# A hybrid RWKV-7 and short-convolution block on one NeuronCore: one pair's recurrence outputs on other array quadrants, weight casts with a higher scheduling priority, and mix splits spread over projection tiles

## The chip, the cores and the metric

The kernel runs on one core of one Trainium2 chip. The metric is the device time of one execution in microseconds (us). The core's engines are named as the profile names them: PE (TensorE, the matmul engine; its weight loads are listed as PEld), DVE (VectorE), ACT (ScalarE), POOL (GpSimd) and SP (SyncE, which here issues nearly all DMAs). A small q behind a name (SPq) means the engine's instruction queue.

## What is computed

The input is 512 tokens of width 2048, with 16 learned tokens put in front (528 rows). The layer normalises the rows, multiplies them by `w_in` (2048 x 8320), and feeds two head groups: 16 RWKV-7 heads of 64 channels, and a gated width-3 convolution over 1024 channels. Cut to what matters:

```python
hn = _rmsnorm(h_res, norm_in_g[l]);  P = hn @ w_in[l]
# RWKV-7 group: token shift, then r, k, v, g_r, decay and a from P
def step(S, inp):                       # per head, S is 64 x 64
    r_t, w_t, k_t, v_t, kk_t, b_t = inp
    sa = einsum('bhvk,bhk->bhv', S, kk_t)
    S = S * w_t[..., None, :] - sa[..., None] * b_t[..., None, :] + v_t[..., None] * k_t[..., None, :]
    return S, einsum('bhvk,bhk->bhv', S, r_t)
yn  = groupnorm_per_head(y) * lnx_g + lnx_b
y_a = (yn + bonus) * silu(g_r)
# convolution group
y_b = Bg * causal_conv3(Cg * hc, conv_w[l]) * silu(g_c)
h_res = h_res + concatenate([y_a, y_b]) @ w_out[l]
out = _rmsnorm(h_res, norm_f_g)[:, 16:]
```

All inputs and the output are float32.

## The kernel before, in words

**Precision.** Every large matmul operand is split into a high part (a cast to fp32r) and a low remainder, and each product is made of three matmuls: high x high, high weight x low input, low weight x high input.

**Weights.** `prefetch` (L130) walks through one list of half tiles, `stream`: the 65 column tiles of `w_in` in the order of `plan`, then `w_out`. For each it takes a raw buffer `wr` (three of them), issues one DMA of 512 KB on SP (L134), and calls `split_w` twice, once per quarter of 512 columns. `split_w` (L123) casts on ACT (`wh`, L126) and subtracts on DVE or POOL (`wl`, L127: POOL takes every second quarter). There are six buffers each for `wh` and `wl`, so a cast waits until PE has done with the quarter six places earlier, and a raw buffer is free again when both its remainders are made.

**Projection.** `mains` (L448) is a Python generator that issues the projection's matmuls (L314) one by one; a tile takes 96 (for k, r, v, g, C and h) or 48 (for B and gc) matmuls in four quarters. After each tile `use` (L376) puts the vector work behind it: scaling, token shift, gates, the convolution. The last tiles of the plan are C, h, B and gc for convolution groups 4 to 7.

**What sets the order.** PE's order is written out by hand: the program's order is PE's order. `fill(ns)` (L500) draws matmuls from the generator until their costed length reaches `ns`, so that other PE work (the preparation, the recurrence) is laid between stretches of projection; `until` (L510) draws until a named tile is done. The lengths are in the table `FW` (L42). `later(ns, fn)` (L481) holds a DMA back until that many costed ns of projection have been drawn, and puts it behind the last weight DMA on SP. On ACT, DVE, POOL and SP a scheduler chooses the order when the program is built: by a cost model of its own it takes, among the instructions that are ready, the one earliest in the program. A block under `tc.high_priority(offset=n)` counts as if it stood n instructions earlier. Once chosen, the order on each engine is fixed, and an engine waits at an instruction whose operands are late, with all behind it. `ahead()` (L532) is such a block with the offset `AHEAD` (600); it holds the few copies that PE needs soon (`pn`, `u`, `st`, and the low-rank tanh and the solve's copies).

**Preparation.** The 16 heads are eight pairs of two. `prepare(i)` (L568) makes a pair's operands: two low-rank products `tz` and `ta` (L514), then `tz + 1` on DVE (L580), a scan `cc` (L582), two exponentials, the products `te`, `bk` (L590, L601) and `ar` (L597, L606), squares and splits (`sq_h`, `rk_h`, L550). PE then makes the Gram matrices `g` (L624). A triangular 16 x 16 solve of 72 blocks runs on DVE (`prod`, `tt`, `y`, L717 to L732); `y` goes to DRAM by a DMA held back by `later` (L747) and comes back as `xT` and `xo` (L738, L739). `invert` (L770) finishes two pairs' inverses (`t`, L790, is its first PE step). The operands of every pair and chunk go to DRAM (`opd`).

**Recurrence.** `recur` (L873) runs over nine chunks (chunk 0 holds the 16 learned tokens); all matmuls in it are 64 x 64 and take one quadrant of the array. For each chunk: `rz` part 0/1 (L887) into two PSUM buffers `z[0]` and `z[1]` of a pool of two, a negated copy `pn` (L895), the solve's product into the second half of the same buffers (L904), its copy `u` (L907, L908), and then two lists of matmuls laid alternately: `here` (L932), the state update `zs`, whose rows and columns of the array are the same half (the diagonal quadrants), 16 items; and `there` (L936), the output `zy`, whose columns are the other half (the off-diagonal quadrants), 24 items, three for each pair. An item is two matmuls, one per head. Then DVE makes the new state (`st`, L942, L943), `norm` (L950) normalises the outputs (DVE L958, L959, L962, L967, ACT L961, POOL L963 and L101, transpose L968) and a `later` puts them into DRAM (`yd`, L972). `fill(p)`, `fill(u)` and `fill(s)` lay projection matmuls between the steps.

**Mix splits and output.** `split_mix(j)` (L996) makes the 16 operand tiles of the output projection. For j below 8 it loads `rb`, `gg` (three buffers each) and two halves of `mr` (four buffers) from `yd` by SP (L1003, L1004, L1007), does two DVE steps (L1010), a cast on ACT (L1015) and a remainder on DVE (L1016). For j from 8 it loads `mr` from `mixd` (L1014), which `use` wrote after the gc tile. Before, `recur` is followed by `fill(last)` of 14000 ns, the held DMAs, and then by a loop over j = 0 to 15: the first eight with no projection between them, the others each after the tile gc j - 8 is done. The output projection (L1054) follows, four column blocks, and the tail (L1141 on) has its order by hand.

Of the kernel before, what the change touches and what calls it, by code (L numbers as in the profile page):

```python
# [9 lines left out]
F32 = mybir.dt.float32  # L10
# [3 lines left out]
ALU = mybir.AluOpType  # L14
AX = mybir.AxisListType
# [3 lines left out]
P = 128  # L19
DM = 2048  # L20
KT = DM // P
# [3 lines left out]
CH = 64  # L25
NCH = SEQ // CH + 1
LP = NCH * CH
NPAIR = 8
# [13 lines left out]

FW = dict(
    evac=34, start=1062, lora=2200, gram=8000, gram_b=13500, gram2=4800, gram3=3500, misc=2000, v=2000, vt=1000, solve=22500, solve_first=26000,
    tr=3200, lev=3000, cp=4200, out=1500, begin=17000, p=2900, u=2900, s=5200, last=14000,
)


AHEAD = 600


def _constants():
# [24 lines left out]
def hymba_kernel(ctx: ExitStack, tc: tile.TileContext, xt, xtok, w_in, w_out, pv, lup, cst, msk, gf, out):  # L77
    nc = tc.nc
# [44 lines left out]
    def split_w(q, rq, eng):  # L123
        hi = wp.tile([P, 512], F32R, tag="hi", name=f"wh{q}", bufs=6)
        lo = wp.tile([P, 512], F32R, tag="lo", name=f"wl{q}", bufs=6)
        nc.scalar.copy(hi, rq)  # L126
        eng.tensor_tensor(out=lo, in0=rq, in1=hi.bitcast(F32), op=ALU.subtract)  # L127
        quarters[q] = (hi, lo)

    def prefetch(upto):  # L130
        while state["next"] < min(upto, len(stream)):
            j = state["next"]
            raw = wp.tile([P, 1024], F32, tag="raw", name=f"wr{j}", bufs=3)
            state["dma"] = nc.sync.dma_start(raw, stream[j]).ins  # L134
            for q in range(2):
                split_w(2 * j + q, raw[:, q * 512 : (q + 1) * 512], nc.gpsimd if q and j > 8 else nc.vector)
            state["next"] = j + 1

    keep = ctx.enter_context(tc.tile_pool(name="keep", bufs=1, side="right"))
# [37 lines left out]
    raw = {}  # L177
# [390 lines left out]
    def prepare(i):  # L568
# [8 lines left out]

        tz = low_rank(i, 0, up, hv[:, 0, i : i + 1], f"tz{i}", -1.0)
        ta = low_rank(i, 1, up, hv[:, 1, i : i + 1], f"ta{i}", 0.0)
        nc.vector.tensor_scalar(out=tz, in0=tz, scalar1=1.0, scalar2=None, op0=ALU.add)  # L580
        cc = tr(f"cc{i}")
        nc.vector.tensor_tensor_scan(cc, smask.rearrange("p c s -> p (c s)"), tz, 0.0, op0=ALU.mult, op1=ALU.add)  # L582
        nc.gpsimd.memset(e1[:, :, 0:1], 1.0)
# [289 lines left out]
    def recur(ch):  # L873
        ops = {}
        load_chunk(ch, 0, range(NPAIR), ops)
        load_chunk(ch, 1, range(NPAIR), ops)
        st = None
        for c in range(NCH):
            last = c == NCH - 1
            z = [pz.tile([P, 2, 4, CH], F32, tag="tz", name=f"rz{c}_{e}") for e in range(2)]  # L880
            for k in range(4):
                for part in range(0 if c else 1, 2):
                    for e in range(2):
                        t = ops[c, 2 * k + e]
                        o = O_KK if part else O_AR
                        for h, hs, ho in heads:
                            nc.tensor.matmul(  # L887
                                z[e][ho if e else hs, 0, k], t[hs, o : o + CH],
                                t[hs, O_V : O_V + CH] if part else st[hs, 4 * e + k],
                                start=(part == 0 or c == 0), stop=(part == 1),  # L890
                            )
            pn = ch.tile([P, 2, 4, CH], F32, tag="pn", name=f"pn{c}", bufs=2)
            with ahead():
                for e in range(2):
                    nc.scalar.activation(pn[:, e], z[e][:, 0], AF.Copy, scale=-1.0)  # L895
            if c and not last:
                load_chunk(ch, c + 1, range(0, 4), ops)
            fill(FW["p"])
            for k in range(4):
                for e in range(2):  # L900
                    t = ops[c, 2 * k + e]
                    for h, hs, ho in heads:
                        m = ho if e else hs
                        nc.tensor.matmul(z[e][hs, 1, k], t[m, O_X : O_X + CH], pn[m, e, k], start=True, stop=True)  # L904
            u = ch.tile([P, 2, 4, CH], F32, tag="u", name=f"u{c}", bufs=2)
            with ahead():
                nc.scalar.copy(u[:, 0], z[0][:, 1])  # L907
                nc.vector.tensor_copy(u[:, 1], z[1][:, 1])  # L908
            if c and not last:
                load_chunk(ch, c + 1, range(4, NPAIR), ops)  # L910
            fill(FW["u"])
            here, there = [], []
            if not last:
                zs = pi.tile([P, NPAIR, CH], F32, tag="misc", name=f"zs{c}")
            if c:
                zy = pi.tile([P, NPAIR, CH], F32, tag="ser", name=f"zy{c}")
            for k in range(4):
                for e in range(2):
                    t, j = ops[c, 2 * k + e], 4 * e + k
                    if not last:  # L920
                        here += [(zs, j, t, O_B, u[:, e, k], 0, 2), (zs, j, t, O_K, t[:, O_V : O_V + CH], 1, 2)]
                    if c:
                        there += [
                            (zy, j, st[:, j], O_AR + CH, t, 0, 3),
                            (zy, j, t[:, O_V : O_V + CH], O_KK + CH, t, 1, 3),
                            (zy, j, u[:, e, k], O_BR, t, 2, 3),
                        ]
            for n in range(max(len(here), len(there))):
                if n < len(here):
                    d, j, t, o, x, a, b = here[n]  # L930
                    for h, hs, ho in heads:
                        nc.tensor.matmul(d[hs, j], t[hs, o : o + CH], x[hs], start=(a == 0), stop=(a == b - 1))  # L932
                if n < len(there):
                    d, j, x, o, t, a, b = there[n]
                    for h, hs, ho in heads:
                        nc.tensor.matmul(d[ho, j], t[hs, o : o + CH], x[hs], start=(a == 0), stop=(a == b - 1))  # L936
            if not last:
                new = ch.tile([P, NPAIR, CH], F32, tag="st", name=f"st{c}", bufs=2)
                scale = dd[:, c].unsqueeze(2).to_broadcast([P, NPAIR, CH])
                with ahead():  # L940
                    if c:
                        nc.vector.tensor_tensor(out=new, in0=zs, in1=st, op=ALU.add)  # L942
                    nc.vector.tensor_tensor(out=new, in0=new if c else zs, in1=scale, op=ALU.mult)  # L943
                st = new
            if c:
                norm(ch, zy, c)
            fill(FW["s"])


    def norm(ch, zy, c):  # L950
        nv = ch.tile([P, 4, NPAIR], F32, tag="nv", name=f"nv{c}", bufs=2)
        yc = ch.tile([P, NPAIR, CH], F32, tag="yc", name=f"yc{c}", bufs=2)
        yt = ch.tile([P, NPAIR * CH], F32, tag="yt", name=f"yt{c}", bufs=2)

        def spread(j):
            return nv[:, j].unsqueeze(2).to_broadcast([P, NPAIR, CH])

        nc.vector.tensor_reduce(out=nv[:, 0], in_=zy, op=ALU.add, axis=AX.X)  # L958
        nc.vector.scalar_tensor_tensor(out=yc, in0=spread(0), scalar=-1.0 / CH, in1=zy, op0=ALU.mult, op1=ALU.add)  # L959
        yq = yt.rearrange("p (j s) -> p j s", s=CH)  # L960
        nc.scalar.activation(yq, yc, AF.Square)  # L961
        nc.vector.tensor_reduce(out=nv[:, 1], in_=yq, op=ALU.add, axis=AX.X)  # L962
        nc.gpsimd.tensor_scalar(  # L963
            out=nv[:, 2], in0=nv[:, 1], scalar1=1.0 / CH, scalar2=LNX_EPS, op0=ALU.mult, op1=ALU.add
        )
        rsqrt(nv[:, 3], nv[:, 2])
        nc.vector.tensor_tensor(out=yc, in0=yc, in1=spread(3), op=ALU.mult)  # L967
        nc.vector.transpose(yt, yc.rearrange("p j s -> p (j s)"))  # L968

        def put():  # L970
            for b in range(4):
                nc.sync.dma_start(  # L972
                    bass.AP(
                        tensor=yd.tensor,
                        offset=yd.offset + (b // 2) * NPAIR * CH * SEQ + (c - 1) * CH + 32 * (b % 2),
                        ap=[[SEQ, 32], [32 * SEQ, 2 * NPAIR], [1, 32]],
                    ),
                    yt[32 * b : 32 * b + 32].rearrange("p (t s) -> p t s", s=32),
                )

        later(10500, put)
# [4 lines left out]
    ph2.close()  # L986
    with tc.tile_pool(name="ch", bufs=1, side="right", reuse_waits="tile") as ch:
        recur(ch)
        fill(FW["last"])
        run_pending(float("inf"))  # L990

    pp = ctx.enter_context(tc.tile_pool(name="pp", bufs=1, side="right", reuse_waits="tile"))
    order = list(range(KT))
# [2 lines left out]
    def split_mix(j):  # L996
# [3 lines left out]
        if j < NPAIR:  # L1000
# [2 lines left out]
            nc.sync.dma_start(rb, rbd[j])  # L1003
            nc.sync.dma_start(gg, gated[j])  # L1004
            for h, hs, ho in heads:
                o = (h * NPAIR + place[j]) * CH
                nc.sync.dma_start(raw[hs], yd[o : o + CH])  # L1007

            for x, w, z, o in ((raw, 0, rb, ALU.mult), (raw, 1, gg, ALU.add)):
# [5 lines left out]
        nc.scalar.copy(mh, raw)  # L1015
        nc.vector.tensor_tensor(out=ml, in0=raw, in1=mh.bitcast(F32), op=ALU.subtract)  # L1016

    for j in order:
        if j >= NPAIR:
            while ("gc", j - NPAIR) not in ready:  # L1020
                step()
        split_mix(j)
    for _ in flow:
        pass
# [194 lines left out]
```

## Time and profile before

| | |
|---|---|
| median of 3 runs | 1066.87 us (1066.67 to 1069.53) |
| the profiled execution, its time | 1066.87 us |
| the profiled execution, its span (first to last instruction) | 1065.1 us |
| granted TensorE clock, mean | 0.994 |
| PE busy | 98% of the span |
| instructions | 23993 |
| DMA, bytes moved | 167.49 MB, mean 157 GB/s |

The profile comes from one execution. In its timelines a row gives start, length (us), engine, line, operation and tiles, the number of merged instructions, and in brackets how long the engine stood idle before it and who released it. In the list of waits a row gives the waiting engine, tile and line, what it waited for, and the total, the number and the longest. In the chain of waits a row is start, length and what the chain went through. In the windows a row is the stretch, its length, then busy time and instruction count of PE, PEld, DVE, ACT and POOL, the granted clock (1.00 is full), the DMA engines' busy share and GB/s. In the answer for one line or one tile a row gives the shortest, median and longest duration in ns, and the first and last start. One fp32 matmul leaves two rows' worth of records, so a 64 x 64 item of two matmuls counts as four. "issue" stands for time in which an engine waited for nothing that the profile shows.

### The profile page before, as it was taken

The page shows a single profiled execution, that of the slowest core. Times are in us where ns is not written, and L with a number is a line of the kernel's source. Part 1 is how long each engine was busy: PE and PEld are TensorE (multiplying, and loading weights), DVE is VectorE, ACT ScalarE, POOL GpSimd, SP SyncE. Part 2 cuts the span into 40 slices and gives each one's busy share as a digit, 9 for nine tenths or more (in the row PEclk, how much of TensorE's full clock was granted, in tenths as well). Part 3 has the DMA queues.
Part 4 walks back from the last instruction along what each step waited for, and adds up shares of the span by engine and source line. Part 5 has one row for each costly group of instructions (what it writes and reads, how often), then busy time and mean ns, then how long its engine had stood idle before and what let it go on. Part 6 is the DMA issues. An engine that isn't in the chain of part 4 may idle for free.

```text
span 1065.1 us, 23993 instructions
## 1 busy us (share of the span) xinstructions
PE 1040.0 (98%) x9973; PEld 950.0 (89%) x9973; DVE 557.2 (52%) x1064; ACT 367.7 (35%) x682; POOL 292.4 (27%) x307
## 2 busy tenths in 40 slices
PE   8999999999999999999999999999999899999996
PEld 6999998999998999989999989898898878888885
DVE  6784964758553767644676552355444842212132
ACT  6553422533233443233443232222222342323232
POOL 0121323223132222231222231323223142424232
PEclk9999999999999999999999999999999999999999
DMA  8455564455653366643457638676745958333314
GB/s 291 137 136 138 142 169 133 128 132 144 172 152 113 107 169 145 147 141 112 124 127 173 176 108 312 215 243 188 224 104 147 244 184 315 82 96 99 99 60 158
DMA packets 182894, 167.49 MB, mean 157 GB/s; under 512 B 120961, under 2 KB 143233, under 8 KB 182401
## 3 DMA queue, kind: packets, MB, share of 16 engines
q1 hardware_dynamic: 182208, 164.90, 54.7%
q8 instruction: 78, 1.28, 0.5%
q10 hardware_dynamic: 576, 1.07, 0.3%
q14 instruction: 32, 0.25, 0.1%
HBM read 129.05 MB, written 36.88 MB: 156 GB/s over the span
## 4 chain that ended last, share of the span: by engine, by line
PE 91%; DVE 3%; DMA 2%; issue 1%; ACT 1%; SPq 0%; POOL 0%; DVEq 0%; ACTq 0%; POOLq 0%
PE o L1054 17%; PE ps_g L314 9%; PE ps_k L314 9%; PE ps_B L314 8%; PE ps_r L314 8%; PE ps_v L314 8%; PE ps_h L314 8%; PE ps_C L314 8%; PE ps_gc L314 8%; PE g L624 2%; PE zs L932 1%; PE zy L936 1%; DVE mr L1010 1%; PE rz L887 1%; PE ps_lora L314 1%
## 5 line engine op out<-in xcount | busy, mean ns | idle before, releaser
L127 POOL TENSOR_TENSOR wl<-wr,wh 128x512 fp32r<-128x512 f32 x150 | 209.3, 1398 | 486.2 <-ACT wh L126 456.5
L126 ACT CAST wh<-wr 128x512 fp32r<-128x512 f32 x312 | 189.4, 619 | 417.9 <-PE o L1054 92.5
L127 DVE TENSOR_TENSOR wl<-wr,wh 128x512 fp32r<-128x512 f32 x162 | 119.0, 738 | 263.0 <-ACT wh L126 261.9
L1054 PE MATMUL o<-wh,m 128*128 128x512 f32 (+1 forms) x484 | 145.3, 384 | 0.0
L1054 PEld LDWEIGHTS o<-wh,m 128*128 128x128 f32 x484 | 89.6, 188 | 21.4
L1054 PE MATMUL o<-wl,m 128*128 128x512 f32 (+1 forms) x242 | 92.6, 389 | 0.0
L314 PE MATMUL ps_g<-xh,wl 128*128 128x258 f32 (+1 forms) x256 | 72.2, 282 | 4.0 <-DVE wl L127 4.0
L314 PE MATMUL ps_k<-xl,wh 128*128 128x264 f32 x256 | 73.1, 286 | 0.0
L314 PE MATMUL ps_v<-xh,wh 128*128 128x264 f32 x256 | 73.1, 286 | 0.0
L314 PE MATMUL ps_r<-xh,wh 128*128 128x258 f32 (+1 forms) x256 | 72.2, 282 | 0.8 <-ACT wh L224 0.8
L314 PE MATMUL ps_k<-xh,wh 128*128 128x264 f32 x256 | 72.9, 285 | 0.0
L314 PE MATMUL ps_h<-xh,wl 128*128 128x258 f32 (+1 forms) x256 | 72.8, 284 | 0.0
L314 PE MATMUL ps_k<-xh,wl 128*128 128x264 f32 x256 | 72.8, 284 | 0.0
L314 PE MATMUL ps_v<-xh,wl 128*128 128x264 f32 x256 | 72.7, 284 | 0.0
L314 PE MATMUL ps_v<-xl,wh 128*128 128x264 f32 x256 | 72.7, 284 | 0.0
L314 PE MATMUL ps_g<-xl,wh 128*128 128x258 f32 (+1 forms) x256 | 72.5, 283 | 0.0
L314 PE MATMUL ps_g<-xh,wh 128*128 128x258 f32 (+1 forms) x256 | 72.3, 282 | 0.0
L314 PE MATMUL ps_h<-xh,wh 128*128 128x258 f32 (+1 forms) x256 | 72.3, 282 | 0.0
L314 PE MATMUL ps_C<-xh,wh 128*128 128x258 f32 (+1 forms) x256 | 72.3, 282 | 0.0
L314 PE MATMUL ps_C<-xh,wl 128*128 128x258 f32 (+1 forms) x256 | 72.2, 282 | 0.0
L314 PE MATMUL ps_h<-xl,wh 128*128 128x258 f32 (+1 forms) x256 | 72.2, 282 | 0.0
L314 PE MATMUL ps_r<-xl,wh 128*128 128x258 f32 (+1 forms) x256 | 72.1, 282 | 0.0
(263 smaller groups left out, 2691.4 us busy)
## 6 DMA issues: line engine op xcount, KB each, us to landing
wr<-in_w_in_dram SPq DMA_DIRECT2D x127, 512.0 KB
ct<-opd SPq DMA_DIRECT2D x64, 288.0 KB
wr<-in_w_out_dram SPq DMA_DIRECT2D x32, 512.0 KB
opd<-ar SPq DMA_DIRECT2D x8, 576.0 KB
opd<-gt SPq DMA_DIRECT2D x16, 288.0 KB
opd<-bt SPq DMA_DIRECT2D x32, 128.0 KB
xres<-in_xtok_dram SPq DMA_DIRECT2D x4, 768.0 KB
out_dram<-xres SPq DMA_DIRECT2D x6, 512.0 KB
```

The source lines that it names most:

```text
L126: nc.scalar.copy(hi, rq)
L127: eng.tensor_tensor(out=lo, in0=rq, in1=hi.bitcast(F32), op=ALU.subtract)
L314: nc.tensor.matmul(ps[r], ww[:, w], xx[:, kt, a:b], start=(kt == 0 and n == 0), stop=(kt == KT - 1 and n == 2))
L624: nc.tensor.matmul(z[h][:, c - c0], bk[hs, c, h : h + 2, :].rearrange("p a s -> p (a s)"), ar[hs, c].rearrange("p a s -> p (a s)"), start= ...
L887: nc.tensor.matmul(z[e][ho if e else hs, 0, k], t[hs, o : o + CH], t[hs, O_V : O_V + CH] if part else st[hs, 4 * e + k], start=(part == 0 ...
L932: nc.tensor.matmul(d[hs, j], t[hs, o : o + CH], x[hs], start=(a == 0), stop=(a == b - 1))
L936: nc.tensor.matmul(d[ho, j], t[hs, o : o + CH], x[hs], start=(a == 0), stop=(a == b - 1))
L1010: nc.vector.scalar_tensor_tensor(out=raw, in0=x, scalar=hl[:, w, j : j + 1], in1=z, op0=o, op1=(ALU.add, ALU.mult)[w])
L1054: nc.tensor.matmul(ps[t + p], mm[:, tk], ww[:, o], start=(jj == 0 and q == 0), stop=(jj == KT - 1 and q == 2))
```

## The change

Five edits, in three parts.

1. In chunks 1 to 8 the three output items of the last pair (place 7) go to the list `here`: state and operands swap roles as stationary and moving operand, and the result goes into the first half of `z[0]` (columns 0 to 63), on the same partitions as the rows. `zy` holds seven pairs instead of eight, `norm` runs its first two DVE steps once for the seven and once for the one, and `split_mix` reads the two heads of that pair in swapped order.
2. `split_w` inside `prefetch` stands under `tc.high_priority(offset=1500)`; `AHEAD` goes from 600 to 3000. The weight DMA itself keeps its place. `tz + 1` in `prepare` moves from DVE to POOL.
3. After the recurrence the splits are laid in another order: j = 8 to 11, each followed by 3700 ns of projection, then the held DMAs, then j = 0 to 7, each followed by 2600 ns, then j = 12 to 15 as their gc tiles are done. The single fill of 14000 ns goes.

```diff
-AHEAD = 600
+AHEAD, WEIGHTS = 3000, 1500
...
-            for q in range(2):
-                split_w(2 * j + q, raw[:, q * 512 : (q + 1) * 512], nc.gpsimd if q and j > 8 else nc.vector)
+            with tc.high_priority(offset=WEIGHTS):
+                for q in range(2):
+                    split_w(2 * j + q, raw[:, q * 512 : (q + 1) * 512], nc.gpsimd if q and j > 8 else nc.vector)
...
-        nc.vector.tensor_scalar(out=tz, in0=tz, scalar1=1.0, scalar2=None, op0=ALU.add)
+        nc.gpsimd.tensor_scalar(out=tz, in0=tz, scalar1=1.0, scalar2=None, op0=ALU.add)
...
-                zy = pi.tile([P, NPAIR, CH], F32, tag="ser", name=f"zy{c}")
+                zy = pi.tile([P, NPAIR - 1, CH], F32, tag="ser", name=f"zy{c}")
...
-                    if c:
+                    if c and j < NPAIR - 1:
                         there += [
                             (zy, j, st[:, j], O_AR + CH, t, 0, 3),
                             (zy, j, t[:, O_V : O_V + CH], O_KK + CH, t, 1, 3),
                             (zy, j, u[:, e, k], O_BR, t, 2, 3),
                         ]
+                    elif c:
+                        here += [
+                            (z[0][:, 0], 0, t, O_AR + CH, st[:, j], 0, 3),
+                            (z[0][:, 0], 0, t, O_KK + CH, t[:, O_V : O_V + CH], 1, 3),
+                            (z[0][:, 0], 0, t, O_BR, u[:, e, k], 2, 3),
+                        ]
...
-                norm(ch, zy, c)
+                norm(ch, (zy, z[0][:, 0, 0:1]), c)
...
-        nc.vector.tensor_reduce(out=nv[:, 0], in_=zy, op=ALU.add, axis=AX.X)
-        nc.vector.scalar_tensor_tensor(out=yc, in0=spread(0), scalar=-1.0 / CH, in1=zy, op0=ALU.mult, op1=ALU.add)
+        for z, j in zip(zs, (slice(0, NPAIR - 1), slice(NPAIR - 1, NPAIR))):
+            nc.vector.tensor_reduce(out=nv[:, 0, j], in_=z, op=ALU.add, axis=AX.X)
+            nc.vector.scalar_tensor_tensor(
+                out=yc[:, j], in0=spread(0)[:, j], scalar=-1.0 / CH, in1=z, op0=ALU.mult, op1=ALU.add
+            )
...
-        fill(FW["last"])
-        run_pending(float("inf"))
...
-                o = (h * NPAIR + place[j]) * CH
+                o = ((1 - h if place[j] == NPAIR - 1 else h) * NPAIR + place[j]) * CH
...
-    for j in order:
-        if j >= NPAIR:
-            while ("gc", j - NPAIR) not in ready:
-                step()
+    for j in range(NPAIR, NPAIR + 4):
+        split_mix(j)
+        fill(FW["last"])
+    run_pending(float("inf"))
+    for j in range(NPAIR):
+        split_mix(j)
+        fill(FW["mix"])
+    for j in range(NPAIR + 4, KT):
+        while ("gc", j - NPAIR) not in ready:
+            step()
         split_mix(j)
```

In the table `FW`, `last` goes from 14000 to 3700 and `mix=2600` is new.

## The prediction

> **What bounds the kernel now.** I read the page's busy times first, then PE's waits, then the chain of waits and the windows at the two places where PE stood still.
>
> ```profile
> span 1065.1 us, 23993 instructions
> PE 1040.0 (98%) x9973; PEld 950.0 (89%) x9973; DVE 557.2 (52%) x1064; ACT 367.7 (35%) x682; POOL 292.4 (27%) x307
> ...
> PE ps_B L314 <- ACT wh L126: 5.8, 1, 5.8
> PE ps_g L314 <- DVE wl L127: 4.0, 3, 1.4
> PE zy L936 <- issue: 2.3, 2, 1.3
> ```
>
> PE is busy 1040.0 of 1065.1 us and no other engine is past 52%, so time is won only by taking PE work away or by ending a PE wait. The waits give three: one of 5.8 us on a weight cast, three of 4.0 us together on a weight remainder, and 2.3 us inside the recurrence's output matmuls. The rest of the idle time lies at the head and the tail, which the change leaves alone. All sums below are against the profiled execution: 1066.87 us, with a span of 1065.1 us; it is also the median of the three runs shown.
>
> **Part 1: pair 7's outputs on the other quadrants.** In each of chunks 1 to 8, L932 issues 16 items (two 64x64 matmuls each, one per head) on the array's diagonal quadrants, and L936 issues 24 on the off-diagonal ones, alternately. The change moves three of the 24 to the other list: 19 and 21.
>
> ```profile
> 675.95 0.23 PE L932 MATMUL zs<-ct 64*64 64x64 f32 x2
> 675.97 0.22 PE L936 MATMUL zy<-ct 64*64 64x64 f32 x2
> ...
> 676.07 0.23 PE L932 MATMUL zs<-u,ct 64*64 64x64 f32 x2
> ...
> 729.70 0.28 PE L936 MATMUL zy<-ct 64*64 64x64 f32 x4
> 729.82 0.28 PE L936 MATMUL zy<-u,ct 64*64 64x64 f32 x4
> ```
>
> A round that holds one item of each list takes 676.07 - 675.95 = 0.12 us; a round with a zy item alone takes 729.82 - 729.70 = 0.12 us too. So the burst's length is the longer list: 24 rounds become 21, 3 x 0.12 = 0.36 us less per chunk, 2.9 us in eight. The bounds are 0 and 2.9. The third row of the waits says why it may be less: twice PE stood in the midst of this burst, 2.3 us together, waiting for nothing the profile shows. The number of instructions is unchanged, so where their supply is the limit a denser burst only meets the gap sooner. I take the six chunks without a gap: **2.2 us**. The Trainium skill (Runtime: NRT & Kernel Launch, "Instruction fetch mechanics") says that the fetch of straight-line code is mostly hidden, because instructions are dispatched more slowly than they are fetched; by that, all eight chunks would gain, 2.9 us. The row of the two gaps speaks against it, without naming their cause.
>
> The new outputs lie in z[0] (rz), whose buffer the next chunk's first matmul needs, so that matmul now also waits for DVE's reads in the normalisation.
>
> ```profile
> 768.14 0.28 PE L936 MATMUL zy<-u,ct 64*64 64x64 f32 x3
> 769.96 0.68 DVE L959 SCALAR_TENSOR_TENSOR yc<-nv,zy 128x512 f32<-128x512 f32 x1
> 774.23 0.34 PE L887 MATMUL rz<-st,ct 64*64 64x64 f32 x8
> 552.66 0.21 DVE L723 TENSOR_REDUCE tt<-prod 72x16 f32<-72x64 f32 x1
> ```
>
> This is the chunk with the least room: DVE has read zy at 770.64, and rz starts at 774.23. Two added small instructions, by the nearest row some 0.2 us each, end near 771.1; 3.1 us are left, room for four wl of 0.69 us in front. Cost: nothing, hidden by the projection matmuls of fill(s). If that cover is gone, PE waits with every rz behind it.
>
> **Part 2: weights' casts first.** The three waits of ps_g have one shape:
>
> ```profile
> 557.79 0.62 ACT L550 CAST rk_h<-r 128x512 fp32r<-128x512 f32 x1 [2.53 <-DVE r L609]
> 558.32 2.70 ACT L126 CAST wh<-wr 128x512 fp32r<-128x512 f32 x5
> ...
> 559.93 2.27 DVE L726 TENSOR_TENSOR prod<-y,tt 72x512 f32<-72x512 f32 x1
> 562.84 1.67 DVE L127 TENSOR_TENSOR wl<-wr,wh 128x512 fp32r<-128x512 f32 x2
> ...
> 563.96 0.39 PE L314 MATMUL ps_g<-xh,wl 128*128 128x258 f32 x1 [1.19 <-DVE wl L127]
> ```
>
> Five casts stood behind the preparation's rk_h on ACT, which itself stood idle for 2.53 us; then the remainders stood behind the y solve's prod on DVE, and PE waited 1.19 us. With splits 1500 program positions ahead, the casts fall into ACT's idle stretches and the remainders ahead of prod: **4.0 us** go (bounds 0 and 4.0). What the splits pass is made later: some three wl of 0.69 us, 2 us on the y solve and on the preparation. The y solve is read late:
>
> ```profile
> 562.94 0.32 SPq L747 DMA_DIRECT2D sx<-y  x1
> 568.47 0.62 ACT L126 CAST wh<-wr 128x512 fp32r<-128x512 f32 x1 [1.85 <-DMA wr<-in_w_in_dram]
> 613.80 1.09 PE t L790 x64
> ```
>
> Its inverse is used by PE at 613.80. But SP stands at that DMA, and weight loads are behind it: 2 us later for y is 2 us later for the cast at 568.47. By then six quarters are cast ahead, and a quarter is 24 matmuls at 0.12 us, 2.9 us of PE, so some 17 us from 563.96; PE needs the next about 581. Hidden. The preparation has less room:
>
> ```profile
> 515.67 0.68 DVE L606 TENSOR_TENSOR ar<-r,e 128x512 f32<-128x512 f32 x1
> 519.63 1.99 PE g L624 x32
> 556.23 0.68 DVE L606 TENSOR_TENSOR ar<-r,e 128x512 f32<-128x512 f32 x1
> 566.96 1.99 PE g L624 x32
> L580 DVE TENSOR_SCALAR tz<-tz x8: 459/461/462, 59.6 to 544.9; 128x576 f32<-128x576 f32 x8
> L594 POOL TENSOR_SCALAR ta<-ta,hv x8: 827/832/1553, 67.1 to 550.4; 128x576 f32<-128x576 f32 x8
> ```
>
> An even pair's last operand is ready 519.63 - 516.35 = 3.3 us before PE's gram, an odd pair's 10 us. In the even pair one wl (0.69 us, at 516.28) can move ahead of ar; two leave 1.9 us. The step tz + 1 moves from DVE (0.46 us) to POOL; the nearest row, a POOL tensor_scalar of the same size, takes 0.83 to 1.55 us, 0.4 to 1.1 us more on the chain, still inside. Below nothing: it frees 8 x 0.46 us of DVE, where no time is to be won. The Trainium skill (SBUF — State Buffer, "Who interferes with whom") speaks against the move: GpSimd and a DVE instruction with two SBUF inputs share a port, and the one that comes second is held for the whole instruction. The row's 1.55 us beside 0.83 us fits that; by the rule the add takes the longer time in the odd pairs, whose 10 us cover it. AHEAD goes from 600 to 3000 so that pn, u and st stay ahead of the splits: nothing, since they are ahead now.
>
> **Part 3: mix splits spread over projection tiles.** The wait of 5.8 us is one queue:
>
> ```profile
> 815.62 0.35 SPq L134
> 817.62 6.10 DMA mr<-yd
> 847.51 5.15 DMA wr<-in_w_in_dram
> 853.43 13.10 PE ps_B L314 x48
> 857.35 0.40 PE L314 MATMUL ps_B<-xh,wh 128*128 128x512 f32 x1
> 866.15 0.39 PE L314 MATMUL ps_B<-xh,wl 128*128 128x512 f32 x1
> ...
> 853.40:858.00 4.60, 4.57 (x12) 3.65 (x13) 4.24 (x6) 3.30 (x6) 1.28 (x1) 0.58 0.90 338
> ```
>
> SP issued a weight load at 815.62 and the next at 847.51. In the 31.9 us between it issued the loads of the mix splits, which stand for a buffer until DVE has done an earlier split. PE lived on what was cast and loaded ahead, ran dry for 5.8 us until 853.43, and then had a granted clock of 0.58: nine matmuls took 857.35 - 853.43 = 3.92 us, where the next 38 took 866.15 - 857.35 = 8.80 us, 0.232 each; nine are 2.08. So the wait cost 5.8 + 1.8 = **7.6 us**.
>
> ```profile
> 803.09 7.08 PE ps_B L314 x30
> ...
> 877.66 177.06 PE o L1054 x798
> ...
> L1010 DVE SCALAR_TENSOR_TENSOR mr<-mr,hl,rb x8: 740/746/752, 823.8 to 846.5; 128x512 f32<-128x512 f32 x8
> ```
>
> The change emits splits 8 to 11 first (from DRAM tiles written long before), one per 3.7 us of projection, then 0 to 7, one per 2.6 us: 14.8 + 20.8 = 35.6 us of matmuls, while PE has 67 us of projection after the recurrence (877.66 - 803.09, less 7.6). Weight loads traced between two splits then stand before the later ones. The splits' own pace on DVE is (846.5 - 823.8) / 7 = 3.2 us, against 2.6 us offered, so SP may lag some 5 us over eight. The hold fell short by 5.8 us at 31.9, so holds up to 26 us cost nothing. 7.6 us go (bounds 0 and 7.6). What is late next: the splits of pairs 0 to 7, done by some 850 as now, and PE reads the first at 877.66 - 13.8, near 864.
>
> **Sum.** 2.2 + 4.0 + 7.6 = 13.8; 1066.87 - 13.8 = **1053.1 us**.
>
> **The rivals.**
> A. The casts still come late. If ps_g waits end on the DMA or on rk_h, part 2 gives nothing: 1057.1. For it: the cast at 568.47 did wait for a load. Against: by then DVE, not DMA, held PE.
> B. SP is still held. The splits' DMAs keep their waits, and if the scheduler's clock runs ahead of DVE's real one, a weight load stays behind several. Full price: 1053.1 + 7.6 = 1060.7. Against: it takes a hold past 26 us, eight splits in a row; the loads now have places between.
> C. A mild form of D, one wait of 6.1 us an even pair: (6.1 - 3.3) x 4 = 11 us, 1064.3.
> D, the other side: **preparation starves**. wl now stands on DVE's queue as soon as the schedule thinks its cast is done, but the cast waits for PE to free a buffer:
>
> ```profile
> DVE wl L127 <- ACT wh L126: 261.9, 103, 6.1
> POOL wl L127 <- ACT wh L126: 456.5, 112, 10.9
> ```
>
> DVE stood up to 6.1 us, POOL up to 10.9 us at such a place, and behind them now stand the scan, te, ar, and on POOL tz + 1, on which the scan waits. Two waits of 6.1 us in an even pair are 12.2 us on 3.3 us of room: 8.9 x 4 = 36 us, 1089. It decides from 3.3 us; to end slower by 0.3% it needs a slip of (13.8 + 3.2) / 4 + 3.3 = 7.6 us per even pair. Against: mean waits are 2.5 and 4.1 us, and g waits for nothing today.
> E. Better: the two gaps of 2.3 us in the recurrence go too, and all eight chunks gain: 1053.1 - 2.3 - 0.7 = 1050.1.
>
> **How the numbers follow.** 0.3% (3.2 us) is about what a measurement of this kernel can tell from no change: 1063.7 to 1070.1 is the same. Forecast 0.60, A 0.12, B 0.11, C 0.06, D 0.05, E 0.06. Faster: forecast, A, B and E, 0.89; same: C, 0.06; slower: D, 0.05. The range reaches from E to B, 1049.9 to 1061, and leaves C and D out.
>
> **What would show it.** Right: L936's and L932's bursts 0.36 us shorter per chunk; no ps_g <- wl in PE's waits; no ps_B <- wh, no clock of 0.58 after the recurrence, and SP's weight loads there never over 26 us apart; PE busy near 1036 (1040.0 less 2.2 and 1.8). Wrong: PE waiting at g L624, at rz L887 for DVE, or at o L1054 for m.

## The result, and the profile after

| | before | after |
|---|---|---|
| median | 1067.07 us (1066.67 to 1069.53, 4 runs) | 1059.74 us (1058.47 to 1061.95, 4 runs) |
| ratio | | 0.9929, 95% interval 0.9904 to 0.9954 |
| the profiled execution: time, span | 1066.87, 1065.1 | 1061.95, 1060.1 |

The change is faster by 7.3 us; 13.8 were forecast. A trace is one execution, in after and in runs 2 and 4 the slowest measured, in runs 6, 9, 10 and 12 the fastest, so that a trace can lie up to 2.7 us from the median of its kernel: the two traces here differ by 5.0 us of span.

First the busy times of the page and PE's waits in the trace of after (engine, tile and line, what it waited for; total, number, longest):

```profile
PE 1039.8 (98%) x9973; PEld 948.8 (89%) x9973; DVE 560.8 (53%) x1072; ACT 365.4 (34%) x682; POOL 305.0 (29%) x315
```

```profile
PE rz L940 <- issue: 2.0, 1, 2.0
...
PE g L625 <- DVE gt L634: 1.5, 3, 0.9
PE ps_B L315 <- DVE wl L127: 1.4, 1, 1.4
...
PE zy L944 <- issue: 0.8, 1, 0.8
PE ps_g L315 <- DVE wl L127: 0.8, 2, 0.4
```

The wait of 5.8 us of ps_B for wh is gone, and of the 4.0 us of ps_g for wl 0.8 are left. Three new rows stand there: g for gt, ps_B for wl, and a gap of 2.0 in the output matmuls (now at an item of pair 7, hence rz). And PE is busy 1039.8 us, not 1036: the busy time that was to go is still spent.

To see where, I cut the span at three points that PE's order gives every version: the rz of chunk 1 (the first row of 64 rz records; chunk 0, which part 1 leaves alone, comes before it), the ps_B tile that follows the recurrence (803.09 in before), and the first o. The chain of waits has them for before (the first row; the other two are in the prediction) and for after:

```profile
667.36 1.09 PE rz L887 x64
```

```profile
671.11 1.09 PE rz L888 x64
...
806.03 10.62 PE ps_B L315 x45
...
872.84 27.31 PE o L1069 x117
```

| stretch | before | after | difference | forecast |
|---|---|---|---|---|
| up to chunk 1 of the recurrence (part 2) | 667.36 | 671.11 | +3.75 | -4.0 |
| recurrence, chunks 1 to 8 (part 1) | 135.73 | 134.92 | -0.81 | -2.2 |
| mix splits (part 3) | 74.57 | 66.81 | -7.76 | -7.6 |
| output and tail | 187.4 | 187.3 | -0.1 | 0 |

Part 3 paid what was forecast, part 1 a third, and part 2, forecast to gain 4.0, lost 3.75. The runs below take these apart; each is read by its ratio and by the same three points. (The number behind a ps_B row, x30 or x45, says how many matmuls the chain merged into it.)

### The profile page after: what moved, and what is told of

Read it like the earlier page. It is cut to its first block, busy times and chain, and to the rows that moved or that the text cites. A ratio compares the mean times of both kernels' runs of the same rounds, so it can differ in the third digit from the quotient of the medians.

```text
span 1060.1 us, 23983 instructions
## 1 busy us (share of the span) xinstructions
PE 1039.8 (98%) x9973; PEld 948.8 (89%) x9973; DVE 560.8 (53%) x1072; ACT 365.4 (34%) x682; POOL 305.0 (29%) x315
## 4 chain that ended last, share of the span: by engine, by line
PE 86%; DVE 6%; DMA 3%; issue 2%; POOL 2%; ACT 1%; SPq 0%; DVEq 0%; ACTq 0%; POOLq 0%
PE o L1069 17%; PE ps_C L315 9%; PE ps_gc L315 9%; PE ps_k L315 9%; PE ps_B L315 8%; PE ps_h L315 8%; PE ps_g L315 6%; PE ps_r L315 6%; PE ps_v L315 6%; DMA wr<-in_w_in_dram 2%; PE zs L940 1%; PE g L625 1%; DMA wq<-in_w_in_dram 1%; PE ps_lora L315 1%; PE rz L888 1%
## 5 line engine op out<-in xcount | busy, mean ns | idle before, releaser
L127 DVE TENSOR_TENSOR wl<-wr,wh 128x512 fp32r<-128x512 f32 x162 | 126.1, 783 | 250.9 <-ACT wh L126 240.9
```

## The experiments

**1. The mix splits alone.** The loop of part 3 on the kernel before, nothing else:

```diff
-    for j in order:
...
+    for j in range(NPAIR, NPAIR + 4):
+        split_mix(j)
+        fill(FW["last"])
```

> Part 3 alone (mix splits spread), the rest as before. Theory of the queue: SP's weight loads no longer stand behind eight splits, so the wait of ps_B of 5.8 us and the half clock after it go: 7.6 us less than before, about 1059.5. Rival (the wait moves to another place, o waiting for m or ps_gc for a cast): gain under 4 us, with a PE wait after 803 us that names it.

Measured: 1058.46 us, ratio 0.9911 (0.9898 to 0.9924). PE's issue gaps and its three points:

```profile
PE zy L936 <- issue: 1.6, 2, 1.0
```

```profile
667.39 1.09 PE rz L887 x64
...
802.46 10.64 PE ps_B L314 x45
...
869.28 30.81 PE o L1058 x132
```

The first stretch is that of before, the mix stretch 869.28 - 802.46 = 66.82, as in after. Part 3 alone gives as much as the whole change or more. The medians lie 9.4 us apart, more than the 7.6 expected; in the trace the mix stretch has 7.75 of them, and another 0.66 lie in the recurrence, which this edit doesn't touch and where the gaps were 1.6 us instead of 2.3.

**2. Pair 7 alone.** Part 1 on the kernel before.

```diff
-                    if c:
+                    if c and j < NPAIR - 1:
...
```

> Part 1 alone (pair 7's outputs on the other quadrants). Theory: each burst is three rounds of 0.12 us shorter, 2.8 us in all, less what the issue gaps take back: a gain of 2 to 2.8 us if the gaps stay at 2.3 us together. Rival (instruction supply sets the burst): bursts shorter by 0.36 us only where no gap falls, gaps longer than before, gain under 1 us.

Measured: 1066.74 us, ratio 0.9986 (0.9978 to 0.9995).

```profile
PE ps_B L314 <- ACT wh L126: 7.9, 1, 7.9
...
PE rz L939 <- issue: 2.0, 1, 2.0
PE zy L943 <- issue: 1.5, 1, 1.5
```

```profile
666.51 1.09 PE rz L887 x64
...
802.03 10.62 PE ps_B L314 x45
```

The ratio is worth 1.5 us (0.5 to 2.3). That lies between the theory, 2 to 2.8, and the rival, under 1; the gaps grew as the rival says. In the trace the recurrence takes 135.52, only 0.2 less than before: eight bursts are 0.36 shorter each, 2.9 together, but the two gaps grew from 2.3 to 3.5, and behind the first the granted clock fell (0.64 from 730 to 734 us), which costs another 4 x (1 - 0.64) = 1.4 there. What little comes out early is waited for at the mix splits, where 5.8 became 7.9.

**3 and 4. The two halves of part 2 alone.** Run 3 has the scheduling priorities on the kernel before, run 4 only the step tz + 1 on POOL:

```diff
+            with tc.high_priority(offset=WEIGHTS):
```

```diff
-        nc.vector.tensor_scalar(out=tz, in0=tz, scalar1=1.0, scalar2=None, op0=ALU.add)
+        nc.gpsimd.tensor_scalar(out=tz, in0=tz, scalar1=1.0, scalar2=None, op0=ALU.add)
```

> The two offsets alone (casts 1500 ahead, AHEAD 3000), tz + 1 still on DVE. Theory formed after the result: the casts behind rk_h are there because the schedule held them not ready, so an offset moves nothing in pairs 2 to 7, the three waits of ps_g stay at 1.2 to 1.4 us each, and the time is within 1 us of before. The step of the prediction: the casts come first, the three waits go, 4 us less.

> tz + 1 on POOL alone, no offsets. Theory: this edit carries all that part 2 did: a wait of some 1.4 us of ps_B near 160 us appears, ps_g's three waits shrink below 0.5 us each, and g waits for gt instead; together 0 to 3 us slower than before. Rival (the offsets do it): none of these waits changes, time as before.

Measured: run 3 1066.87 us, ratio 0.9991 (0.9982 to 1.0001); run 4 1070.13 us, 1.0014 (1.0001 to 1.0027). The waits of ps_g in run 3, then PE's waits of run 4 and its first rz:

```profile
PE ps_g L315 <- DVE wl L127: 4.0, 3, 1.4
```

```profile
PE ps_B L314 <- ACT wh L126: 7.7, 2, 6.5
PE g L624 <- DVE gt L633: 2.7, 3, 1.4
```

```profile
671.83 1.09 PE rz L887 x64
```

The priorities leave the three waits as they were: 4.0. (Run 3's rz of chunk 1 is at 668.48, 1.1 later than before, all of it gathered in the first 26 us.) The new waits that the trace of after shows up to chunk 1 come with tz: with it alone rz is at 671.83, 4.5 later than before, and g waits for gt. In the eight traces with tz on DVE and all remainders in their place rz is at 666.5 to 668.5, in the two with tz on POOL at 671.1 and 671.8. By its ratio run 4 loses 1.5 us (0.1 to 2.9).

The named waits of PE up to there are as long in after as in before, so they alone don't make 3.75. At the same instruction of PE, after is behind before by 0.6 us at 25 us, and from there loses 1.6 at ps_B (158 us), 0.8, 1.4 and 0.8 at g in three odd pairs and 1.5 in half clock behind the second of these, and gains 2.8 back at the three ps_g.

How tz does so is seen in one odd pair, before and after. ACT, DVE and POOL of before:

```profile
391.05 0.46 DVE L580 TENSOR_SCALAR tz<-tz 128x576 f32<-128x576 f32 x1
...
391.55 1.36 DVE L582 TENSOR_TENSOR_SCAN cc<-smask,tz 128x576 f32<-128x576 f32 x1
```

```profile
404.24 0.62 ACT L550 CAST rk_h<-r 128x512 fp32r<-128x512 f32 x1 [2.53 <-DVE r L609]
404.76 2.69 ACT L126 CAST wh<-wr 128x512 fp32r<-128x512 f32 x5
```

and of after, where PE is 2.1 us later at this place already:

```profile
391.68 1.66 POOL L581 TENSOR_SCALAR tz<-tz 128x576 f32<-128x576 f32 x1 [2.74 <-DMA opd<-vs]
393.68 1.28 POOL L127 TENSOR_TENSOR wl<-wr,wh 128x512 fp32r<-128x512 f32 x1 [0.33 <-ACT wh L126]
```

```profile
393.78 1.20 DVE L727 TENSOR_TENSOR prod<-y,tt 72x8 f32<-72x8 f32 x1
...
395.49 1.34 DVE L583 TENSOR_TENSOR_SCAN cc<-smask,tz 128x576 f32<-128x576 f32 x1
```

```profile
408.52 0.62 ACT L551 CAST rk_h<-r 128x512 fp32r<-128x512 f32 x1 [3.80 <-DVE r L610]
409.04 2.18 ACT L126 CAST wh<-wr 128x512 fp32r<-128x512 f32 x4
...
419.62 1.14 ACT L126 CAST wh<-wr 128x512 fp32r<-128x512 f32 x2 [2.86 <-DMA wr<-in_w_in_dram]
```

```profile
420.27 0.69 DVE L127 TENSOR_TENSOR wl<-wr,wh 128x512 fp32r<-128x512 f32 x1 [1.28 <-ACT wh L126]
420.88 2.75 DVE L634 TENSOR_TENSOR gt<-g,cs 128x512 f32<-128x512 f32 x5
```

```profile
422.82 0.97 PE L625 MATMUL g<-ar,bk 64*128 64x128 f32 x3 [0.94 <-DVE gt L634]
```

The scan starts 3.94 later, 1.8 more than PE's own delay. The longer time of tz, 1.66 us on POOL instead of 0.46 on DVE, is not what does it here: tz starts earlier on POOL, which is free, and ends at 393.34, where before's end with PE's 2.1 added is 393.6. But the scan now starts 2.14 after tz's end, not 0.03: DVE's fixed order has solve steps in front of it, among them the prod at 393.78, which took 1.20 us beside a remainder on POOL, where prod steps of this shape took 0.16 in before. In the even pairs the scan follows tz at once, and there the longer time counts, 1.2 to 1.3 us. On ACT rk_h is 4.28 later and waits 3.80 instead of 2.53, and the casts still stand behind it. Casts that are late give their raw buffers back late, so a weight load lands late (the wait for DMA at 419.62), wl behind it, gt behind wl on DVE, and PE waits at g. The first half of the chain, up to rk_h, is the same in the odd pairs 3, 5 and 7; the second half is read from this pair alone. That the step as a whole costs time, runs 4, 5 and 11 show.

**5 and 11. The change without part 2, and without tz alone.** Run 5 is parts 1 and 3; run 11 is the whole change with tz + 1 left on DVE.

> The kernel before with part 1 (pair 7 on the other quadrants) and part 3 (mix splits spread), and nothing of part 2. Theory, that part 2 as a whole costs time because tz + 1 on POOL delays the casts it was meant to bring forward: 1055.7 to 1057.5 us, that is 1.0 to 2.8 below the 1058.46 of part 3 alone, and 2 to 4 below the whole change; no wait of PE at L624 for gt, three waits of ps_g for wl, 4.0 us together. Rival, that part 1 gives nothing once the wait on the mix splits is gone because the issue gaps in the output bursts grow by as much: 1058 to 1059, with more than 3 us of issue gaps.

> The whole change, but tz + 1 stays on DVE. Theory, that all of what part 2 costs is this one step and its offsets do nothing: as e5, 1056.5 to 1058 us, with the three waits of ps_g for wl, 4.0 us, back, and without the waits of g for gt and of ps_B for wl. Rival, that the offsets themselves move the casts and remainders: the three waits stay gone, 1053 to 1054.

Measured: run 5 1057.34 us, ratio 0.9899 (0.9885 to 0.9913); run 11 1056.92 us, 0.9904 (0.9891 to 0.9918). They can't be told apart, and both lie 0.25 to 0.3% under the 0.9929 of the whole change, with intervals that still overlap its own. The first rz of run 11 stands where that of before does:

```profile
PE ps_g L315 <- DVE wl L127: 4.0, 3, 1.4
```

```profile
667.55 1.09 PE rz L888 x64
```

Both expectations of the theory held: the priorities do nothing here either, and tz on POOL accounts for part 2's loss, 2.4 to 2.8 us by the medians. The two points around the recurrence in run 5:

```profile
666.91 1.09 PE rz L887 x64
...
800.76 10.63 PE ps_B L314 x45
```

The recurrence takes 133.85 in run 5 and 132.96 in run 11 (667.55 to 800.51): part 1 gives more here than in after and run 2, though the gaps are 3.4 and 2.5 us. The difference is the half clock behind the first gap, which these two traces don't have.

**6. The operand loads kept out of the burst.** The gaps fall where SP issues the next chunk's loads. On run 5, a one-element write that needs pn now precedes each load, and all eight loads of a chunk stand at one place (the second call, for pairs 4 to 7, goes):

```diff
-                load_chunk(ch, c + 1, range(0, 4), ops)
+                load_chunk(ch, c + 1, range(NPAIR), ops, pn)
...
+                nc.gpsimd.tensor_copy(t[0:1, 0:1], after[0:1, 0, 0, 0:1])
```

> As e5, but the loads of the next chunk's operands wait for the first copy (pn) of the chunk, so that none starts in the output matmuls of the chunk before. Theory, that the issue gaps come while these loads are issued and landing: no issue gap over 0.5 us at the zs and zy lines, 1.5 to 3 us less than e5. Rival, that the gaps belong to the place in the program (so many instructions of the kind in a row): the gaps stay at the same two chunks, time within 0.5 us of e5.

Measured: 1061.28 us, ratio 0.9944 (0.993 to 0.9957), slower than run 5. Its second gap on PE, and SP before it:

```profile
785.72 0.21 PE L943 MATMUL zy<-u,ct 64*64 64x64 f32 x1 [2.71 <-issue]
```

```profile
775.97 3.78 SPq L870 DMA_DIRECT2D ct<-opd  x8
```

The theory fell: with the loads issued by 779.75 a gap of 2.71 us still comes at 783.0, longer than any before, though in another chunk. The plain rival fell too, since one of the gaps moved. The recurrence takes 3.2 us more than in run 5: half clock follows the second gap, and the rz of chunks 2 to 8 take 0.1 to 0.3 us longer.

**7 and 8. The casts put ahead by hand.** On run 5; run 7 forces the order on ACT in the odd pairs, run 8, on run 7, also gives the one remainder that PE waits for to POOL:

```diff
-        nc.scalar.copy(hi, rq)
+        state["cast"] = nc.scalar.copy(hi, rq).ins
...
+        with tc.issue_after(state["cast"]) if p else ExitStack():
+            rh, rl = split(r, f"rk{i}", SEQ)
```

```diff
+    late = [2 * plan.index(("g", j)) for j in (2, 4, 6)]
...
-nc.gpsimd if q and j > 8 else nc.vector)
+nc.gpsimd if q and j > 8 or j in late else nc.vector)
```

> As e5, but in the odd pairs the copy rk_h stands on ACT behind the weight casts that are written ahead of it, by hand. Theory, that the casts behind rk_h are the whole of the three waits of ps_g: they go, 3 to 4 us less than e5. Rival, that DVE's queue holds PE as much, since the remainder wl still stands behind the y solve's last product of 2.27 us and sum: the waits shrink only by what rk_l took in front of wl, 0.68 each, to some 2 us together, and the time by 1.5 to 2.

> As e7, and the one remainder that PE waits for in these pairs is made by POOL instead of DVE, so that neither rk_h on ACT nor the y solve on DVE stands before it. Theory of both queues: the three waits of ps_g go wholly, 3.5 to 4.5 us less than e5, near 1053. Rival: POOL's three remainders in a row (1.9 us each beside DVE's two-input products) are late themselves, and PE waits for POOL at the second or third: no faster than e7.

Measured: run 7 1057.0 us, ratio 0.9898 (0.9885 to 0.9912), the time of run 5; run 8 1052.45 us, 0.9855 (0.9842 to 0.9869). Run 7's wait of ps_g, then ACT and DVE in its last pair:

```profile
PE ps_g L314 <- DVE wl L127: 2.9, 3, 1.2
```

```profile
555.48 2.17 ACT L126 CAST wh<-wr 128x512 fp32r<-128x512 f32 x4
559.02 0.62 ACT L550 CAST rk_h<-r 128x512 fp32r<-128x512 f32 x1 [1.38 <-DVE r L609]
```

```profile
557.28 1.66 DVE L609 SCALAR_TENSOR_TENSOR r<-r,hv,ta 128x512 f32<-128x512 f32 x1
558.86 2.16 DVE L718 TENSOR_TENSOR prod<-d,y 72x512 f32<-72x512 f32 x1
...
563.58 1.28 DVE L127 TENSOR_TENSOR wl<-wr,wh 128x512 fp32r<-128x512 f32 x2
```

The casts now run at 555.48, before rk_h, yet wl starts at 563.58 behind the same y solve (at 562.84 in before): DVE's queue held PE too. The waits fell by 1.1 us only, less than either side expected, and the time not at all. POOL started its remainders earlier, at 556.69, and beside them DVE's r took 1.66 us (0.74 in run 1) and the first prod 2.16 (1.06); the second prod, now behind them, took 1.17 (2.27), so that r's 0.9 is what DVE lost. In run 8 there is no row of ps_g waiting for wl, and the first stretch shrinks:

```profile
552.73 6.01 POOL L128 TENSOR_TENSOR wl<-wr,wh 128x512 fp32r<-128x512 f32 x3 [3.87 <-ACT wh L127]
```

```profile
662.80 1.09 PE rz L889 x64
```

667.36 - 662.80 = 4.6 us, and 4.1 against the 666.91 of run 5: the 4.0 that part 2 was to give, got by moving both queues. Three remainders take 6.01 us on POOL, slow but early enough.

**9, 10 and 12. PE's stream shifted.** In before, after and runs 1 to 5, 7, 8 and 11 the two gaps come at the same instruction of PE's program (after 143 and 153 records of the burst without part 1, 144 and 155 with it), although PE is there at times up to ten us apart (726.31 in run 8, 736.08 in run 4). So, on run 8, I moved PE's stream by replacing warm-up matmuls at the start, whose results nobody reads. This is run 12; runs 9 and 10 replace one and two larger warm-up matmuls by 41 and 82 of the small ones:

```diff
-    nc.tensor.matmul(pwarm[:, 0:P], cold[:, 0:P], cold[:, 0:P], start=True, stop=True)
+    for n in range(7):
+        a = b = 64 * (n % 2)
+        nc.tensor.matmul(pwarm[b : b + 64, 0:64], cold[a : a + 64, 0:64], cold[a : a + 64, 0:64], start=True, stop=True)
```

> As e8, but one of the two 128x512 warm-up matmuls at the start, whose results nobody reads, is replaced by 41 of 64x64, so that every later PE instruction stands 40 places further on in PE's stream. Theory, that an issue gap belongs to a place in PE's instruction stream: the two gaps of e8 (at 726.31, after 144 records of its burst, and at 762.13, after 155) come 40 matmuls, 80 records, earlier: after some 64 and 75 records of the same bursts; time within 1 us of e8. Rival, that they belong to the burst itself (its buffers, its loads): they stay after 144 and 155 records.

> As e8, but both 128x512 warm-up matmuls are replaced by 82 of 64x64, a shift of 80 places. Theory of the place in the stream: 160 records earlier than 144 and 155 lies ahead of both bursts, in projection matmuls, where a late instruction has more time; these two gaps go, up to 3.1 us less than e8 (1049.4) unless a place of another chunk is shifted into its burst. Rival as in e9: the gaps stay, 1052 to 1053.

> As e8, but the 128x128 warm-up matmul is replaced by 7 of 64x64, a shift of 6 places (12 records). Theory, that a gap stands where PE's stream passes a fixed boundary right after a dense stretch (e8 to e10: gaps only at records 132 to 159 of a burst of 160, and none of the two left when the stream was shifted by 40 or 80 places): the two gaps come at records 132 and 143 of the same bursts instead of 144 and 155, each within 1 us of its size in e8; time within 1 us of e8. Rival, that the place within the burst sets it: still at 144 and 155. Third case, that they go as in e9: then how far the stream is shifted does not set where they come, and the cause stays open.

Measured: run 9 1051.01 us, ratio 0.9853 (0.9838 to 0.9868); run 10 1050.26 us, 0.9851 (0.9837 to 0.9865); run 12 1050.26 us, 0.984 (0.9826 to 0.9853). Run 9 keeps one gap, in a projection tile; run 10 one of 0.89 us, late in the burst of another chunk; run 12 none in the recurrence. The gap row of run 9, and the ends of the recurrence in run 12:

```profile
709.81 0.29 PE L318 MATMUL ps_C<-xh,wh 128*128 128x258 f32 x1 [1.17 <-issue]
```

```profile
663.52 1.09 PE rz L891 x64
...
793.62 10.62 PE ps_B L317 x45
```

Both gaps of run 8 went with each of the three shifts, so the burst itself does not cause them: nothing in it was changed, and ACT, DVE, POOL and SP run the same instructions in the same order in all four traces. But they did not move by as many records as the stream did, as my theory had it; a shift of 12 records was enough to lose them. That the place in PE's instruction stream matters is shown, as far as one trace of each version can show it (single executions of runs 9 and 10 took up to 1053.1 us, as long as run 8, and were not traced); which rule makes a place bad is open.

The traces go further on what ends a gap. Their DMA records have packets of 16 KB of the kind "instruction" on queue q8, some 7 us apart here. From chunk 1 to the end of the recurrence 13 traces have 24 gaps, 0.6 to 2.7 us long, and 22 of them end 2.2 to 2.7 us after such a packet has started (the first gaps of runs 1 and 4 end 3.5 and 3.8 after one). In run 6 PE stands from 783.01, and the packet starts only at 783.46; the DMA view of 783.40 to 783.50 has it:

```profile
q8 instruction: 1, 0.02, 58.6%
```

The gap ends at 785.72. So PE waited for instructions that were fetched late: that is the reading that fits nearly every gap, though no run changed the fetch itself. Without gaps the recurrence takes 793.62 - 663.52 = 130.10, 5.6 less than before. Against run 8 the profile of run 12 gains 2.8 us, the ratios of 9 and 10 nothing that can be told, that of 12 some 0.15% with intervals that still touch.

Run 12, at 0.984, has the lowest ratio measured, ahead of both kernels; runs 9 and 10 can't be told from it.

## Why the prediction was right in part

The time came out inside the range and the sign was right, but half of the sum did not come, and part 3 carried it alone. That 1059.7 is still inside is luck: the range reached to 1061 for rival B, whose mechanism (SP still held) did not come, and the 6.5 us that are missing were lost in parts 1 and 2.

- **Part 3, 7.6 forecast, 7.76 measured.** Reading right: one queue, SP's, dry PE, then half a clock. In after SP has weight loads at 816.74, 831.22, 841.78, 846.06 and 856.45, nowhere 26 us apart, and PE is busy through the whole mix stretch at a granted clock of 1.00 (first row of the last fence of this section). Rival B did not come.
- **Part 1, 2.2 forecast, 0.81 in after, 0.2 in run 2 and 1.2 between runs 1 and 5** (135.07 to 133.85). 0.36 per burst was right. The step that failed is "I take the six chunks without a gap": it took the two gaps to stay at 2.3 us with nothing behind them. They grew, in after to 2.8, and in after and run 2 a half clock behind the first gap cost 3.41 x (1 - 0.50) = 1.7 more (last row of that fence). Without part 1 the recurrence takes 135.07 to 135.73; with it, and with PE's stream unshifted, 134.92 and 135.52 where the half clock came and 132.96 to 133.85 where it did not (runs 5, 7, 8, 11). So the 2.2 were about right without the half clock, and the prediction had no term for it. It had said that a denser burst meets the gap sooner, and priced that at two bursts only. The Trainium skill (Runtime: NRT & Kernel Launch, "Instruction fetch mechanics") has the fetch mostly hidden; run 12 shows the recurrence as if it were, -5.6, the runs on the unshifted stream do not. That is about the size of rival E's gain, 2.9 + 2.3.
- **Part 2, -4.0 forecast, +3.75 in the trace of after, 2.4 to 2.8 lost by the medians of runs 5 and 11.** Two steps failed. "With splits 1500 program positions ahead, the casts fall into ACT's idle stretches": run 3 shows the offset to change nothing. The likely reason is that the scheduler picks among what it thinks ready, and had these casts ready only after rk_h: four of them stand before rk_h in the program, where run 7 could put rk_h behind them, so they would have come first without any offset had they been ready by its clock. That clock is not in the traces. A priority ranks; it can't make a thing ready. And "the add takes the longer time in the odd pairs, whose 10 us cover it": the 10 us lay between the last operand and the gram, and the gram was covered; but the casts hung on the same chain earlier, by rk_h, and they had no room at all. rk_h is 4.28 us later, 2.2 beyond PE's own delay. The add's time was mis-sized too, and not by the neighbour: it takes 1.66 to 1.69 us in all eight pairs, also where DVE stands idle beside it (at 351.62 in after), so the 0.83 to 1.55 of the nearest row did not carry over. The Trainium skill's rule on the shared port (SBUF — State Buffer, "Who interferes with whom"), which the prediction weighed and took as covered, agrees with the prod that took 1.20 us beside POOL's remainder; tz's 1.66 us it does not explain.
- **Rivals.** A had the mechanism (casts behind rk_h) with a gain of zero for part 2; nobody had the loss. D's starving of the preparation showed in small, 1.5 us at g, though by late casts and not by its wl waiting in front of the scan.
- **What would show it.** PE waiting at g was named as a sign against, and it came. The forecast of PE busy at 1036 missed in the main because two new stretches of half clock, 3.4 us lost, took back more than the one that went had cost, 1.8. The mix stretch of after, and these two:

```profile
806.03:872.84 66.81, 66.81 (x383) 58.52 (x383) 44.32 (x61) 24.03 (x42) 22.84 (x16) 1.00 0.73 211
...
424.76:428.16 3.40, 3.40 (x18) 3.40 (x17) 1.12 (x2) 1.25 (x3) 0.16 (x1) 0.50 1.11 308
...
735.38:738.78 3.40, 3.40 (x17) 3.40 (x17) 2.34 (x6) 0.63 (x1) 0.00 (x0) 0.50 0.98 337
```

In the last two windows (the granted clock stands third from the end) PE is busy all the time and gets half as much done.

## What to carry to other kernels

Before a priority is counted on, ask whether the scheduler thinks the instruction ready at all; if not, only an order written by hand moves it, and it must move on every queue between it and the waiter, as runs 7 and 8 show. A step that is moved to another engine is priced by where the next step then falls in its own queue, and by all that hangs on the result on other engines, here a cast and through it the weight stream, not by the nearest use on the critical engine. Where gains are counted per burst, the stalls inside the bursts belong to the sum with their own change, and with the half clock that may follow them.

## What was not expected of the hardware

- A gap of PE in a dense burst of 64x64 matmuls comes at the same instruction in ten versions and goes when 7 small matmuls in place of one, some 720 us earlier, shift the stream; nearly every gap ends 2.2 to 2.7 us after an instruction packet has started. Any edit to PE's program may thus win or lose 2 to 3 us of a trace here that have nothing to do with it.
- A short idle time can be followed by half clock, and the same one need not be: behind the 2.02 us before 734.80 in after, PE ran at half clock; behind the 2.06 before 730.64 in run 5 it didn't. What decides is, in the main, how the idle time falls on a grid. In each trace half clock starts on one grid of 3.41 us, at a phase of its own, and lasts one or more whole cells (the last of a trace is cut off by its end): in after at 21.98, 424.75 and 735.37, which are 118 and 91 cells apart. The cell before the last of these in after, and the cell of run 5 that has most of its gap:

```profile
731.96:735.36 3.40, 1.38 (x75) 1.21 (x65) 1.39 (x2) 0.00 (x0) 0.00 (x0) 1.00 0.91 303
```

```profile
729.12:732.52 3.40, 1.88 (x27) 1.81 (x27) 1.94 (x5) 0.00 (x0) 0.00 (x0) 1.00 1.06 364
```

All 2.02 us fall into one cell of after; run 5's gap is cut into 0.54 and 1.52. Over all traces, from 26 us to the output's end, an idle time that puts 1.88 us or more into one cell (the first gap of run 2 and the second of run 6 among them) is followed by half clock in the next, and at full clock one that puts 1.52 or less there is not, with two exceptions, both at g: 0.94 us in after and 1.44 in run 4 were enough. So idle time is not the whole rule, and what g has that the bursts don't was not tried.
